# One block-inverse solve behind keys times state in a chunked delta rule, and 512-column products over [high | low] token sums in a feed-forward layer

## The chip, the cores and the metric

The kernel runs on one NeuronCore of a Trainium2 chip. Its engines work side by side and meet through semaphores: TensorE (PE, matrix products into PSUM), VectorE (DVE), ScalarE (ACT), GpSimd (POOL), and SyncE (SP), which issues most of the transfers. The metric is the device time of one execution in microseconds (us).

## The reference, cut to what matters

One layer of a streaming encoder on 512 tokens of width 1024, all in fp32: a half-step SwiGLU feed-forward (d_ff = 2816), a token mixer, a second half-step feed-forward. Each starts with an adaptive RMS norm; each result is added to x under a gate. Half of the mixer is latent attention, the other half a gated delta rule with 4 heads of 128 x 128 state, in chunks of 64 tokens in the reference (the kernel takes 128). The parts that the change touches:

```python
def _swiglu(h, w_in, w_out):
    gate, up = jnp.split(h @ w_in, 2, axis=-1)
    return (jax.nn.silu(gate) * up) @ w_out
...
    M = A + jnp.eye(CHUNK, dtype=A.dtype)
    rhs = jnp.concatenate([v * beta[..., None], k * (beta * jnp.exp(G))[..., None]], axis=-1)
    W = lax.linalg.triangular_solve(M, rhs, left_side=True, lower=True, unit_diagonal=True)
    u, wk = W[..., :GDN_DV], W[..., GDN_DV:]
...
    def step(state, inp):
        u_c, wk_c, qd_c, kd_c, qk_c, gl_c = inp
        v_new = u_c - jnp.einsum('bhck,bhkv->bhcv', wk_c, state)
        o_c = jnp.einsum('bhck,bhkv->bhcv', qd_c, state) + jnp.einsum('bhcs,bhsv->bhcv', qk_c, v_new)
        state = state * gl_c[..., None, None] + jnp.einsum('bhck,bhcv->bhkv', kd_c, v_new)
        return state, o_c
```

So u = M⁻¹(beta v), wk = M⁻¹(beta e^G k), and v_new = u − wk·S. By linearity v_new = M⁻¹(beta v − beta e^G (k·S)) as well.

## The kernel before, in words

**Arithmetic.** Every large product is made of three matmuls (mm3, L264 to L269): each operand x is kept as a high part xh, x cast to fp32r (a rounded fp32), and a low part xl = x − xh; the product is wh·xh + wh·xl + wl·xh. ACT makes the casts (L193, L804), DVE the low parts (L198, L809).

**Stages.** The first feed-forward with its down projection runs to about 410 us of the span, the mixer's projections, convolutions, attention and block inverses to about 615, the recurrence and the output projection to about 680, the second feed-forward from there to the end.

**The recurrence** (`solve`, `recur`, `gated_out`, and the loop at the end of the mixer). The kernel works on NB = 4 blocks of 128 tokens. inv[p] is the inverse of block p (its last products are L1639 and L1642). `solve(p)` computes uu = inv·vb (L1685) and, for p > 0, w = inv·kbg (L1694), both copied to SBUF; kbg and kd are scaled copies of the keys. `recur(p)` computes pw = w·S (L1711), vn = uu − pw (L1713), pq = q·S (L1719), and after a yield the state's update pst = kd·vn (L1726), S = Sg + pst (L1731; Sg, the decayed state, is made by POOL), po = qk·vn (L1734), and o = o + po (L1738). `gated_out(p)` normalises o: squares hn on ACT (L1772), their sums gs on DVE (L1773), ve (L1748), an inverse root ry on POOL (L179), on = o·ry (L1232), then four transposes of on on PE (L1757) and three operations for each head that store the high and low parts mh, ml. Beside it `fill` issues the output projection over rows that are ready (L267 to L269 with mh, ml): fill.step(3) at each yield of recur, which is nine 512-column matmuls. The loop runs with `matmuls_in_order`: PE's matmuls stay in the written order, the other engines' work is ordered by the scheduler. Each engine runs its own list strictly in order.

**The second feed-forward** (`ffn2_rest`). 22 column tiles of the hidden layer: 4 are done plainly, 18 in a fast scheme that saves an eighth of the products: with the tokens in two halves and the width in two halves, a gate and an up tile (a "pair") take 7 half-size products instead of 8. Its operands are sums of weights (x, y from g and u, `sums`), and sums of tokens t1 to t4 (`token_sums`, made once). Each product is 4 k-steps of three 256-column matmuls (L872, L873, L874). Results lie in two PSUM tiles of 512 columns, A and BC; ACT copies A out at three moments (`early_copy`, L816), DVE adds BC (`both` L822, `gate0` L825, L832), then SiLU, products and splitting. A table of due steps sets the order: pairs start 7 steps apart, their weights are loaded 11 steps ahead, their products stand at steps 0, 1, 3, 4, 6, 9 and 12, and between them stand k-steps of the down projection (512 columns, L267 to L269 with ah, al) as fill. All engines keep the written order here (`in_order`). PSUM has 3 banks of `acc` (names pa) and 5 of `aux` (names pb).

## Time and profile before

| | |
|---|---|
| time, median of 3 runs | 1047.45 us (1047.32 to 1048.46) |
| the profiled execution | 1047.25 us; span 1045.6 us |
| PE busy | 1029.0 us, 98% of the span, 6379 matmuls |
| DVE busy | 682.6 us, 65% |
| ACT busy | 448.6 us, 43% |
| POOL busy | 48.2 us, 5% |
| granted TensorE clock | 0.999 |

The span is the time between the first and the last instruction of the profile; 1.65 us of the execution lie around it. A row of a timeline gives the start in us, the duration in us, the engine, the line, and the tiles (out <- in); in brackets stands how long the engine had been idle and what released it. A row of the windows view gives a stretch, its length, and for PE, weight loads, DVE, ACT and POOL the busy time and the number of instructions, then the granted clock and the DMA share.

### The profile page before, as it was taken

What the parts mean: (1) busy time and instruction counts of PE and PEld (TensorE: products, weight loads), DVE (VectorE), ACT (ScalarE), POOL (GpSimd) and SP (SyncE); (2) the same over time, 40 slices, a digit from 0 to 9 for tenths busy, and PEclk for the clock granted to TensorE, in tenths of its full rate; (3) what the DMA queues carried; (4) which work ended last, traced back from release to release, by engine and by line L of the source; (5) the groups of instructions that cost most, each with busy time, mean ns of one, the idle gap of its engine ahead of it and who ended that gap; (6) DMA issues with size and microseconds to landing.
All of it is one profiled execution on the core that took longest, in us unless ns stands there. A gap on an engine that the chain in (4) does not pass through costs nothing.

```text
span 1045.6 us, 16109 instructions
## 1 busy us (share of the span) xinstructions
PE 1029.0 (98%) x6379; PEld 882.2 (84%) x6379; DVE 682.6 (65%) x1251; ACT 448.6 (43%) x781; POOL 48.2 (5%) x113
## 2 busy tenths in 40 slices
PE   6999999999999999999999999999999999999998
PEld 4778878788887799888778779998999999999986
DVE  4488984333486636648878556788778778777633
ACT  4343222232222226749565464465345444344422
POOL 1000000000000011100010111310000000000000
PEclk9999999999999999999999999999999999999999
DMA  9989973323586439712212201173423334333222
GB/s 274 292 232 322 298 218 101 100 84 94 190 285 220 155 102 231 185 40 54 69 41 56 72 22 41 41 162 101 141 81 102 104 99 121 91 92 109 74 61 81
DMA packets 203689, 136.88 MB, mean 131 GB/s; under 512 B 13777, under 2 KB 186590, under 8 KB 203614
## 3 DMA queue, kind: packets, MB, share of 16 engines
q1 hardware_dynamic: 202318, 131.14, 42.6%
q0 software_dynamic: 1296, 4.72, 2.4%
q8 instruction: 50, 0.82, 0.3%
q14 instruction: 25, 0.20, 0.1%
HBM read 128.63 MB, written 2.49 MB: 125 GB/s over the span
## 4 chain that ended last, share of the span: by engine, by line
PE 90%; ACT 4%; DVE 4%; issue 1%; DMA 1%; POOL 0%; SPq 0%; POOLq 0%; ACTq 0%; DVEq 0%
PE pa L267 20%; PE pa L268 20%; PE pa L269 20%; PE pb L872 6%; PE pb L873 6%; PE pb L874 6%; PE pb L267 1%; PE pb L268 1%; PE pb L269 1%; PE pb L1909 1%; PE pb L418 1%; PE pb L1939 1%; PE pb L1494 1%; DVE cv L1438 1%; PE pb L1912 1%
## 5 line engine op out<-in xcount | busy, mean ns | idle before, releaser
L267 PE MATMUL pa<-hh,wh 128*128 128x512 f32 (+1 forms) x565 | 216.8, 384 | 0.4 <-ACT hh L465 0.4
L193 ACT CAST wh<-wr 128x1024 fp32r<-128x1024 f32 (+1 forms) x106 | 107.9, 1018 | 250.6 <-PE pa L268 177.8
L268 PE MATMUL pa<-hl,wh 128*128 128x512 f32 (+1 forms) x565 | 214.7, 380 | 0.5 <-DVE hl L457 0.3
L269 PE MATMUL pa<-hh,wl 128*128 128x512 f32 (+1 forms) x565 | 214.5, 380 | 0.0
L198 DVE TENSOR_TENSOR wl<-wr,wh 128x1024 fp32r<-128x1024 f32 (+1 forms) x97 | 114.2, 1178 | 104.0 <-ACT wh L193 101.6
L267 PE MATMUL pa<-ah,wh 128*128 128x512 f32 (+1 forms) x396 | 145.5, 368 | 0.6 <-DVE xT L899 0.4
L268 PE MATMUL pa<-al,wh 128*128 128x512 f32 (+1 forms) x396 | 144.5, 365 | 0.0
L269 PE MATMUL pa<-ah,wl 128*128 128x512 f32 (+1 forms) x396 | 143.5, 362 | 0.0
L267 PEld LDWEIGHTS pa<-hh,wh 128*128 128x128 f32 x565 | 106.4, 188 | 23.9 <-issue 3.3
L269 PEld LDWEIGHTS pa<-hh,wl 128*128 128x128 f32 x565 | 106.3, 188 | 20.6 <-issue 0.9
L268 PEld LDWEIGHTS pa<-hl,wh 128*128 128x128 f32 x565 | 106.5, 188 | 19.6 <-DVE hl L457 1.1
L269 PEld LDWEIGHTS pa<-ah,wl 128*128 128x128 f32 x396 | 74.8, 189 | 12.0
L267 PEld LDWEIGHTS pa<-ah,wh 128*128 128x128 f32 x396 | 75.2, 190 | 10.3 <-ACT wh L193 1.7
L268 PEld LDWEIGHTS pa<-al,wh 128*128 128x128 f32 x396 | 75.2, 190 | 7.2
L577 DVE SCALAR_TENSOR_TENSOR aa<-ar,sc,aa 128x512 f32<-128x512 f32 x98 | 72.9, 747 | 8.2 <-DMA ar<-in_w_ada 6.8
L872 PE MATMUL pb<-fh,wh 128*128 128x256 f32 x144 | 40.7, 283 | 0.0
L874 PE MATMUL pb<-fh,wl 128*128 128x256 f32 x144 | 40.7, 283 | 0.0
L874 PE MATMUL pb<-hh,wl 128*128 128x256 f32 x144 | 40.7, 283 | 0.0
L873 PE MATMUL pb<-fl,wh 128*128 128x256 f32 x144 | 40.7, 282 | 0.0
L873 PE MATMUL pb<-hl,wh 128*128 128x256 f32 x144 | 40.7, 282 | 0.0
L899 DVE SCALAR_TENSOR_TENSOR xT<-pa,mod,xT 128x512 f32<-128x512 f32 (+1 forms) x40 | 29.3, 735 | 17.3 <-PE pa L269 17.3
L872 PE MATMUL pb<-hh,wh 128*128 128x256 f32 x144 | 40.6, 282 | 0.0
(445 smaller groups left out, 2003.1 us busy)
## 6 DMA issues: line engine op xcount, KB each, us to landing
wr<-in_ffn_w_in SPq DMA_DIRECT2D x82, 512.0 KB, 3.9
ar<-in_w_ada SPq DMA_DIRECT2D x48, 512.0 KB, 6.1
wr<-in_ffn_w_out SPq DMA_DIRECT2D x34, 512.0 KB, 3.9
ar<-in_w_ada SPq DMA_DIRECT2D x48, 256.0 KB, 4.8
wr<-in_w_in SPq DMA_DIRECT2D x21, 512.0 KB, 4.3
wr<-in_ffn_w_out SPq DMA_DIRECT2D x17, 384.0 KB, 3.4
wl<-wr POOLq DMA_DIRECT2D x9, 512.0 KB, 6.1
wr<-in_w_out SPq DMA_DIRECT2D x8, 512.0 KB, 3.8
```

Of the source, the lines that this page charges most:

```text
L193: self.nc.scalar.copy(hi, raw)
L198: self.nc.vector.tensor_tensor(out=lo, in0=raw, in1=hi.bitcast(F32), op=ALU.subtract)
L267: mm(out, wh, xh, start=start, stop=False)
L268: mm(out, wh, xl, start=False, stop=False)
L269: mm(out, wl, xh, start=False, stop=stop)
L418: nc.tensor.matmul(pg[32 * q:32 * q + 32, :256], self.sc[:, kc:kc + 1].to_broadcast([P, 32]), a[:, kc], start=(e == 0), stop=(e == 1), til ...
L577: nc.vector.scalar_tensor_tensor(out=acc, in0=a, scalar=sc, in1=acc, op0=ALU.mult, op1=ALU.add)
L872: mm(out, wh, xh, start=start and k == 0, stop=False, **kw)
L873: mm(out, wh, xl, start=False, stop=False, **kw)
L874: mm(out, wl, xh, start=False, stop=stop and k == 3, **kw)
L899: nc.vector.scalar_tensor_tensor(out=self.xT[t][:, ts], in0=p[:, ts], scalar=gate[:, t:t + 1], in1=self.xT[t][:, ts], op0=ALU.mult, op1=AL ...
L1438: nc.vector.scalar_tensor_tensor(out=a[:, d:], in0=p[:, :NT - d], scalar=wj(3 - d), in1=a[:, d:], op0=ALU.mult, op1=ALU.add)
```

## The change

**Mixer.** w = inv·kbg is not computed any more, nor are kbg and kd. `recur(p)` multiplies the keys with the state (pk = kT·S, L1722), DVE forms r = e^G·pk − vb for each head (L1724), and one solve follows: pu = inv·r (L1704); ACT copies −pu out as vn. kt is scaled in place where the values are made. A block thus has three yields for p > 0 and two for p = 0, and fill advances by 1, 3 and 2 units at them instead of 3 each.

**Second feed-forward.** The token sums are stored as [high | low], 256 columns each, in one tile. For the four products over token sums (s2, s3, s1, gate1) one 512-column matmul wh·[high | low] (L901) and one 256-column matmul wl·high (L902) take the place of three. The tile's two halves are added afterwards (`fold`, L832). The PSUM tiles are now A, U and G; U lies in `acc` for odd pairs. u's low part is made by ACT (negated copy) and an accumulating transfer on POOL's queue, g1's and the activation's low part, and one fold, by POOL instead of DVE.

```diff
@@ token_sums
-        fh, fl = self.slot(F32R, "fh"), self.slot(F32R, "fl")
-        for name, part in zip(names, (lo, hi)):
-            self.T[name].append((fh[:, part], fl[:, part]))
-        nc.scalar.copy(fh, t)
-        yield
-        v.tensor_tensor(out=fl, in0=t, in1=fh.bitcast(F32), op=ALU.subtract)
+        both = [self.slot(F32R, "fb") for _ in range(2)]
+        for name, x, part in zip(names, both, (lo, hi)):
+            self.T[name].append((x[:, lo], x[:, hi], x))
+            nc.scalar.copy(x[:, lo], t[:, part])
+        yield
+        for x, part in zip(both, (lo, hi)):
+            v.tensor_tensor(out=x[:, hi], in0=t[:, part], in1=x[:, lo].bitcast(F32), op=ALU.subtract)
@@ pair_tasks
                 nc.scalar.copy(r[name + "h"], r[src][:, part])
+                if name in 'u':
+                    nc.scalar.activation(r[name + "l"], r[src][:, part], AF.Copy, scale=-1.0)
+                    nc.gpsimd.dma_start(r[name + "l"].bitcast(F32), r[src][:, part], accum_op=ALU.add)
             return go
 
         def lo(name, src, part=slice(0, 2 * NT)):
             def go():
-                v.tensor_tensor(out=r[name + "l"], in0=r[src][:, part], in1=r[name + "h"].bitcast(F32), op=ALU.subtract)
+                if name not in 'u':
+                    eng = nc.gpsimd if name == "g1" else v
+                    eng.tensor_tensor(out=r[name + "l"], in0=r[src][:, part], in1=r[name + "h"].bitcast(F32), op=ALU.subtract)
             return go
 
         def early_copy(name, part):
             def go():
                 if name not in r:
                     r[name] = self.slot(s=name)
-                nc.scalar.copy(r[name][:, part], r["A"][:, :HALF])
+                out = r[name][:, part]
+                nc.scalar.copy(out, r["A"][:, L])
+                if name == "uc":
+                    fold(out, out, r["A"][:, H])
+                elif part is H:
+                    nc.scalar.copy(r["uc"][:, H], r["A"][:, H])
+                    nc.gpsimd.tensor_tensor(out=out, in0=out, in1=r["uc"][:, H], op=ALU.add)
             return go
 
+        def fold(out, a, b):
+            v.tensor_tensor(out=out, in0=a, in1=b, op=ALU.add)
+
         def both():
-            v.tensor_tensor(out=r["cc"], in0=r["cc"], in1=r["BC"], op=ALU.add)
+            for x in (L, H):
+                fold(r["cc"][:, H], r["cc"][:, H], r["G"][:, x])
+            fold(r["cc"][:, L], r["cc"][:, L], r["U"][:, L])
 
         def gate0():
-            v.tensor_tensor(out=r["uc"][:, H], in0=r["uc"][:, L], in1=r["BC"][:, H], op=ALU.add)
+            fold(r["uc"][:, H], r["uc"][:, L], r["G"][:, L])
+            fold(r["uc"][:, H], r["uc"][:, H], r["G"][:, H])
...
         def act1():
-            v.tensor_tensor(out=r["cc"][:, H], in0=r["cc"][:, H], in1=r["A"][:, :HALF], op=ALU.mult)
+            fold(r["uc"][:, H], r["uc"][:, H], r["A"][:, L])
+            v.tensor_tensor(out=r["cc"][:, H], in0=r["cc"][:, H], in1=r["uc"][:, H], op=ALU.mult)
...
         def act_low():
             al = self.slot(F32R, "al")
-            v.tensor_tensor(out=al, in0=r["cc"], in1=r["ah"].bitcast(F32), op=ALU.subtract)
+            eng = nc.gpsimd if f < FT - 2 else v
+            eng.tensor_tensor(out=al, in0=r["cc"], in1=r["ah"].bitcast(F32), op=ALU.subtract)
@@ product
         if "A" not in r:
-            r["A"], r["BC"] = self.aux(), self.aux()
+            r["A"] = self.aux()
+        if what == "up1":
+            r["U"] = self.acc() if r["odd"] else self.aux()
+        if what == "s3":
+            r["G"] = self.aux()
...
-            mm(out, wh, xh, start=start and k == 0, stop=False, **kw)
-            mm(out, wh, xl, start=False, stop=False, **kw)
+            if both is None:
+                mm(out, wh, xh, start=start and k == 0, stop=False, **kw)
+                mm(out, wh, xl, start=False, stop=False, **kw)
+            else:
+                mm(wide, wh, both, start=start and k == 0, stop=False, **kw)
             mm(out, wl, xh, start=False, stop=stop and k == 3, **kw)
@@ values, solve, recur
+            if p < NB - 1:
+                self.mul(h4(self.kt[p]), h4(self.kt[p]), self.bc(self.kcd[:, 4 * p:4 * p + 4], 4))
...
-        if p > 0:
-            kbg = self.slot(s="kbg")
-            self.mul(h4(kbg), h4(kt), self.bc(self.eG[:, c4], 4))
-        if p < NB - 1:
-            self.kd[p] = self.slot(s="kd")
-            self.mul(h4(self.kd[p]), h4(kt), self.bc(self.kcd[:, c4], 4))
...
-            nc.tensor.matmul(pu[:, hs(h)], u[:, hs(h)], vb[:, hs(h)], start=True, stop=True)
-        self.us[p] = self.slot(s="uu")
-        nc.scalar.copy(self.us[p], pu)
...
-        pw = self.aux()
-        for h in range(4):
-            nc.tensor.matmul(pw[:, hs(h)], kbg[:, hs(h)], u[:, hs(h)], start=True, stop=True)
-        self.wk[p] = self.slot(s="w")
-        nc.scalar.copy(self.wk[p], pw)
+            hs = slice(h * P, (h + 1) * P)
+            nc.tensor.matmul(pu[:, hs], u[:, hs], rhs[:, hs], start=True, stop=True)
+        nc.scalar.activation(vn, pu, AF.Copy, scale=scale)
+        return vn
...
-            vn = self.us[p]
+            vn = self.solve(p, self.vb[p], 1.0)
         else:
-            pw = self.aux()
+            eg = lambda h: self.eG[:, 4 * p + h:4 * p + h + 1]
+            pk, r = self.aux(), self.slot(s="r")
             for h in range(4):
-                nc.tensor.matmul(pw[:, hs(h)], self.wk[p][:, hs(h)], S[:, hs(h)], start=True, stop=True)
-            vn = self.slot(s="vn")
-            nc.vector.tensor_tensor(out=vn, in0=self.us[p], in1=pw, op=ALU.subtract)
+                nc.tensor.matmul(pk[:, hs(h)], kT[h][:, ts], S[:, hs(h)], start=True, stop=True)
+            for h in range(4):
+                nc.vector.scalar_tensor_tensor(out=r[:, hs(h)], in0=pk[:, hs(h)], scalar=eg(h), in1=self.vb[p][:, hs(h)],
+                                               op0=ALU.mult, op1=ALU.subtract)
...
+            yield
+            vn = self.solve(p, r, -1.0)
         yield
...
-                nc.tensor.matmul(pst[:, hs(h)], self.kd[p][:, hs(h)], vn[:, hs(h)], start=True, stop=True)
+                nc.tensor.matmul(pst[:, hs(h)], self.kt[p][:, hs(h)], vn[:, hs(h)], start=True, stop=True)
@@ the mixer's loop
-        chain.add(solving())
...
-        while self.wk[1] is None or deltas.open or deltas.todo:
+        while self.inv[0] is None or deltas.open or deltas.todo:
...
-                for _ in self.recur(p):
+                for i, _ in enumerate(self.recur(p, kT)):
                     loosely(chain, 2)
                     loosely(rest, 4)
                     if not rest.open and not rest.todo:
-                        fill.step(3)
+                        fill.step((1, 3, 2)[i])
                     gated.step(2)
```

**Where instructions move.** First PE, recurrence, block 2: the rows ahead of the four transposes of block 1's on. Before (nine fill matmuls between the last of pq = q·S and the transposes; between po of block 1 and these rows stand nine more, and w·S and q·S):

```order
L1719 MATMUL pb_6127<-S_6090,cv_4729 128x128
L267 MATMUL pa_6102<-mh_5666,wh_5912 128x512
L268 MATMUL pa_6102<-ml_5667,wh_5912 128x512
L269 MATMUL pa_6102<-mh_5666,wl_5913 128x512
L267 MATMUL pa_6102<-mh_5670,wh_5912 128x512
L268 MATMUL pa_6102<-ml_5671,wh_5912 128x512
L269 MATMUL pa_6102<-mh_5670,wl_5913 128x512
L267 MATMUL pa_6149<-mh_5182,wh_6050 128x512
L268 MATMUL pa_6149<-ml_5183,wh_6050 128x512
L269 MATMUL pa_6149<-mh_5182,wl_6051 128x512
L1757 MATMUL pb_6155<-ident_92,on_6153 128x128 x4
L1726 MATMUL pb_6173<-vn_6123,kd_5956 128x128 x4
```

Now (three fill matmuls between q·S and the transposes; between po of block 1 and these rows stand six, and k·S and q·S):

```order
L1731 MATMUL pb_6072<-S_6029,cv_4729 128x128
L267 MATMUL pa_6047<-mh_5186,wh_5938 128x512
L268 MATMUL pa_6047<-ml_5187,wh_5938 128x512
L269 MATMUL pa_6047<-mh_5186,wl_5939 128x512
L1771 MATMUL pb_6086<-ident_92,on_6084 128x128 x4
L1704 MATMUL pb_6104<-r_6061,U_5568 128x128 x4
L267 MATMUL pa_6047<-mh_5669,wh_5938 128x512
L268 MATMUL pa_6047<-ml_5670,wh_5938 128x512
L269 MATMUL pa_6047<-mh_5669,wl_5939 128x512
```

Nine of the eighteen fill matmuls between po and the transposes are gone from there, and the solve r·U stands behind the transposes.

Second, DVE at the same place, from the new state S to on. Before:

```order
L1731 TENSOR_TENSOR S_6090<-Sg_6038,pb_6085 128x512 [waits Pool_49]
L2121 SCALAR_TENSOR_TENSOR xT_106<-pa_6055,mod_1794,xT_106 128x512 [waits PE_49]
L1773 TENSOR_REDUCE gs_6109<-hn_6110 128x4 [waits Activation_49]
L1713 TENSOR_TENSOR vn_6123<-uu_5965,pb_6118 128x512 [waits PE_49]
L1748 SCALAR_TENSOR_TENSOR ve_6113<-gs_6109,oe_5223 128x4 [waits DVE_49]
L1232 TENSOR_TENSOR on_6153<-o_6030,ry_6115 128x512 [waits Pool_49]
L2121 SCALAR_TENSOR_TENSOR xT_106<-pa_6102,mod_1794,xT_106 128x512 [waits PE_49]
L198 TENSOR_TENSOR wl_6309<-wr_6307,wh_6308 128x1024 [waits DMAHW4_49,Activation_49]
```

Now:

```order
L1745 TENSOR_TENSOR S_6029<-Sg_5972,pb_6024 128x512 [waits PE_49,Pool_49]
L1752 TENSOR_TENSOR o_5961<-o_5961,pb_6031 128x512 [waits PE_49]
L2127 SCALAR_TENSOR_TENSOR xT_106<-pa_6014,mod_1794,xT_106 128x512 [waits PE_49]
L198 TENSOR_TENSOR wl_6270<-wr_6268,wh_6269 128x1024 [waits DMAHW2_49,Activation_49]
L1787 TENSOR_REDUCE gs_6051<-hn_6052 128x4 [waits Activation_49]
L1724 SCALAR_TENSOR_TENSOR r_6061<-pb_6060,eG_4081,vb_5460 128x128 [waits PE_49]
L1762 SCALAR_TENSOR_TENSOR ve_6055<-gs_6051,oe_5223 128x4 [waits DVE_49]
L1724 SCALAR_TENSOR_TENSOR r_6061<-pb_6060,eG_4081,vb_5460 128x128 x3
L1260 TENSOR_TENSOR on_6084<-o_5961,ry_6057 128x512 [waits Pool_49]
```

xT and the low part wl of a later weight tile moved ahead of the sums gs, and the first row of r ahead of ve.

Third, PE in the last pair: behind its product s1 (y with the last token sum) the down projection's last parts. Before, from s1's last matmul on:

```order
L874 MATMUL pb_9792<-fh_6924,yl_9728 128x256
L267 MATMUL pa_9902<-ah_9655,wh_9830 128x512
L268 MATMUL pa_9902<-al_9678,wh_9830 128x512
L269 MATMUL pa_9902<-ah_9655,wl_9831 128x512
L267 MATMUL pa_9902<-ah_9807,wh_9830 128x512
L268 MATMUL pa_9902<-al_9827,wh_9830 128x512
L269 MATMUL pa_9902<-ah_9807,wl_9831 128x512
L267 MATMUL pa_9938<-ah_9329,wh_9868 128x512 [waits Activation_49]
L268 MATMUL pa_9938<-al_9352,wh_9868 128x512
L269 MATMUL pa_9938<-ah_9329,wl_9869 128x512 [waits DVE_49]
```

Now:

```order
L902 MATMUL pb_9669<-fb_6909,yl_9613 128x256
L267 MATMUL pa_9772<-ah_9538,wh_9709 128x512
L268 MATMUL pa_9772<-al_9566,wh_9709 128x512
L269 MATMUL pa_9772<-ah_9538,wl_9710 128x512
L267 MATMUL pa_9772<-ah_9683,wh_9709 128x512
L268 MATMUL pa_9772<-al_9706,wh_9709 128x512
L269 MATMUL pa_9772<-ah_9683,wl_9710 128x512
L267 MATMUL pa_9809<-ah_9226,wh_9745 128x512 [waits DVE_49,Activation_49]
L268 MATMUL pa_9809<-al_9254,wh_9745 128x512
L269 MATMUL pa_9809<-ah_9226,wl_9746 128x512
```

The eighth row's accumulator begins with a wait for DVE now: its bank is that of U of this last pair, which is free after this row of DVE (the last one here), the third of the folds of `both`:

```order
L832 TENSOR_TENSOR uc_9608<-uc_9608,pb_9618 128x256 [waits DVE_49]
L1046 TENSOR_TENSOR wl_9783<-wr_9690,wh_9782 128x768 [waits DMAHW5_49,Activation_49]
L854 TENSOR_TENSOR cc_9543<-cc_9543,uc_9608 128x256
L832 TENSOR_TENSOR cc_9688<-cc_9688,pb_9748 128x256 [waits Pool_49]
L832 TENSOR_TENSOR cc_9688<-cc_9688,pb_9748 128x256 [waits DVE_49]
L832 TENSOR_TENSOR cc_9688<-cc_9688,pa_9693 128x256
```

These folds wait for POOL's fold of cc, which waits for two copies by ACT, which wait for s1.

More of the change, by code (lines that the diff above doesn't have):

```diff
@@ L2004, in mixer @@
         self.inv, self.ready64 = [None] * NB, [None] * NB
-        self.kd, self.us, self.o, self.wk = ([None] * NB for _ in range(4))
+        self.o = [None] * NB
         self.S = None
@@ L2041, in mixer @@
         deltas.add(self.values(vT))
-        def solving():
-            solves = Side(wide=2)
-            solves.add(*(self.solve(p) for p in range(NB)))
-            while solves.open or solves.todo:
-                solves.step(2)
-                yield
-        chain.add(solving())
         self.dense_units(4, Rates(sides, (1, 0.75, 2)), 1, z_done)
```

40 lines of the change are left out of this document (16 added, 24 removed).

## The prediction

> **What bounds the kernel now.** I read the page first, then the busy time by stretches of the span, then timelines where PE is not the whole story. From the page, the engines and the chain that ended last:
>
> ```profile
> PE 1029.0 (98%) x6379; PEld 882.2 (84%) x6379; DVE 682.6 (65%) x1251; ACT 448.6 (43%) x781; POOL 48.2 (5%) x113
> PE 90%; ACT 4%; DVE 4%; issue 1%; DMA 1%; POOL 0%; SPq 0%; POOLq 0%; ACTq 0%; DVEq 0%
> ```
>
> PE carries the span. The windows view shows whether it does so in the stages that change (recurrence, its end, then second feed-forward; columns: stretch, length, busy PE, PEld, DVE, ACT, POOL, clock, DMA):
>
> ```profile
> 615.00:660.00 45.00, 44.59 (x325) 37.24 (x326) 28.45 (x58) 20.49 (x47) 5.99 (x5) 1.00 0.12 36
> ...
> 820.00:860.00 40.00, 40.00 (x278) 37.28 (x277) 30.05 (x41) 17.70 (x29) 0.00 (x0) 1.00 0.36 107
> ...
> 980.00:1020.00 40.00, 40.00 (x255) 36.27 (x253) 17.66 (x27) 12.53 (x23) 0.00 (x0) 1.00 0.20 60
> ```
>
> PE is full in all three, so work taken from PE counts, and so does every wait of PE that did not exist. DVE at 75% (30.05 of 40) has room; POOL is idle in the feed-forward. "Busy" is no price, though, as PE's timeline there shows:
>
> ```profile
> 830.77 0.28 PE L872 MATMUL pb<-fh,yh 128*128 128x256 f32 x1
> 830.89 0.28 PE L873 MATMUL pb<-fl,yh 128*128 128x256 f32 x1
> 831.00 0.28 PE L874 MATMUL pb<-fh,yl 128*128 128x256 f32 x1
> ...
> 832.08 0.28 PE L874 MATMUL pb<-fh,yl 128*128 128x256 f32 x1
> 832.20 0.40 PE L267 MATMUL pa<-ah,wh 128*128 128x512 f32 x1
> 832.43 0.40 PE L268 MATMUL pa<-al,wh 128*128 128x512 f32 x1
> 832.67 0.39 PE L269 MATMUL pa<-ah,wl 128*128 128x512 f32 x1
> 832.90 0.28 PE L872 MATMUL pb<-hh,wh 128*128 128x256 f32 x1
> ```
>
> A 256-column matmul lasts 0.28 us but the next starts 0.119 us later (twelve from 830.77 to 832.20: 1.43 / 12). A 512-column one lasts 0.40 and the next starts 0.233 later (832.20 to 832.90: 0.70 / 3). Durations overlap; starts are the price.
>
> **The change part by part.** *1. The products with kbg go.* PE's rows for them, and po of block 1, which I need below:
>
> ```profile
> 627.97 1.06 PE L1694 MATMUL pb<-U,kbg 128*128 128x128 f32 x8
> 628.78 0.47 PE L267 MATMUL pa<-mh,wh 128*128 128x512 f32 x1
> ...
> 635.21 1.95 PE L1694 MATMUL pb<-U,kbg 128*128 128x128 f32 x16
> 636.91 0.47 PE L267 MATMUL pa<-mh,wh 128*128 128x512 f32 x1
> ...
> 644.30 1.06 PE L1734 MATMUL pb<-vn,qk 128*128 128x128 f32 x8
> 645.11 0.47 PE L267 MATMUL pa<-mh,wh 128*128 128x512 f32 x1
> ```
>
> From start to the next start: 0.81 + 1.70 = 2.5 us, with the joints 2.6 at most. Keys times state and r's solve cost what w·S and uu's product did. **−2.6 us.** The copies of w, the subtraction and the scalings that go lie on ACT and DVE, beside PE.
>
> *2. Wide products.* Four products of 18 pairs, 4 k-steps each: 288 times three narrow matmuls (3 × 0.119 = 0.358) become a wide and a narrow (0.233 + 0.119 = 0.352, or with the 0.116 that the first narrow one after a wide one shows at 832.90 rounded 0.349). 288 × (6 to 10 ns) = 1.7 to 2.9; I take the upper end, **−2.8 us**, with −1.4 to −4.4 as ends (5 ns either way, the rounding of a start). The columns stay 768 for a k-step; only one start in three goes.
>
> [...]
>
> DVE per pair: the low parts of u (1.22), g1 (0.69) and the activation (0.69) go, folds come. PE per pair takes 84 × 0.119 + 24 × 0.233 = 15.6 us (8 k-steps of fill), DVE 30.05 / 40 × 15.6 = 11.7. The rows:
>
> ```profile
> L809 DVE TENSOR_TENSOR wl<-wr,wh 128x1024 fp32r<-128x1024 f32 x18 | 21.9, 1218 | 0.2 <-ACT wh L804 0.2
> L841 DVE TENSOR_TENSOR al<-cc,ah 128x512 fp32r<-128x512 f32 x18 | 12.4, 690 | 1.9 <-ACT ah L837 0.7
> L832 DVE TENSOR_TENSOR cc<-cc,pb 128x256 f32<-128x256 f32 x18 | 7.4, 412 | 2.8 <-PE pb L874 2.8
> L816 ACT COPY cc<-pb 128x256 f32<-128x256 f32 x36 | 13.2, 367 | 5.7 <-PE pb L874 5.5
> L481 POOL TENSOR_TENSOR na<-na,sq 128x256 f32<-128x256 f32 x9 | 7.8, 868 | 112.0 <-ACT sq L479 111.9
> L196 POOL DMA_DIRECT2D wl<-wr x9 | 7.9, 878 | 36.1 <-ACT wl L195 36.1
> ```
>
> Off DVE −2.60, on it about four more folds of 0.41 (+1.7): about 10.8 of 15.6. POOL gets 0.88 (issue) + 0.87 (fold) + two 512-column subtractions. In the middle of a pair the new waits (A's halves, G, U's bank) have 3 to 7 steps, over 5 us of other products, before PE needs them: nothing, unless DVE or POOL falls behind (rival below).
>
> *3. PE stalls in the recurrence.* The transposes of on stand in PE's list before the solve, and half of the fill between po and them is gone. How long po to on takes is in the timeline for block 1:
>
> ```profile
> 645.39 0.69 DVE L1738 TENSOR_TENSOR o<-o,pb 128x512 f32<-128x512 f32 x1
> ...
> 646.17 0.63 ACT L1772 ACTIVATE hn<-o 128x512 f32<-128x512 f32 x1 [0.91 <-DVE o L1738]
> ...
> 647.46 0.68 DVE L1773 TENSOR_REDUCE gs<-hn 128x4 f32<-128x512 f32 x1
> ...
> 648.96 0.15 DVE L1748 SCALAR_TENSOR_TENSOR ve<-gs,oe 128x4 f32<-128x4 f32 x1
> 649.19 1.01 POOL L179 TENSOR_TENSOR ry<-ve,mhalf 128x4 f32<-128x4 f32 x1 [1.19 <-DVE ve L1748]
> ...
> 650.23 0.69 DVE L1232 TENSOR_TENSOR on<-o,ry 128x512 f32<-128x512 f32 x1 [1.12 <-POOL ry L179]
> 650.39 1.06 ACT L193 CAST wh<-wr 128x1024 fp32r<-128x1024 f32 x1
> ...
> 651.50 1.22 DVE L198 TENSOR_TENSOR wl<-wr,wh 128x1024 fp32r<-128x1024 f32 x1
> ```
>
> From po's start at 644.30: o after 1.09, hn 0.78 later, gs at best 0.70 later (here DVE was late), 0.70 for gs, 0.23 to ry, 1.04 to on, 0.88 to the transposes (651.11): 5.4 us. PE's cover is now po 0.81, six fill matmuls 1.40, k·S 0.89 and q·S 0.81, three fills 0.78: 4.7. It was 6.8. So blocks 1 and 2 stall 0.7 each; block 0 keeps nine fills there and stalls not; the last block has 0.81 + 15 fills (3.50) = 4.3 and stalls 1.1. For block 1 the cast of a weight tile (1.06) stands before hn on ACT, and xT and wl (1.22) before gs, one r row (0.3) before ve: gs starts 1.5 later and ve 0.3, 1.8 more. Sum 0.7 + 1.8 + 0.7 + 1.1 = 4.3, less the one stall there now:
>
> ```profile
> 659.85 0.66 PE L1757 MATMUL pb<-ident,on 128*128 128x128 f32 x4 [0.41 <-DVE on L1232]
> ```
>
> **+3.9 us**; ends: +0.5 if a fill more or a faster chain covers the plain blocks and half the detour, +5.5 if the detour happens in two blocks. Queued behind PE's wait are the solve, the fill and all later products.
>
> *4. Join of inverses and recurrence.* A copy Y by ACT stands between L1639 and L1642; before, two fill matmuls cover each (the row below: 0.37 for the copy; L1642 starts 0.67 after it starts). Now two of the four have none:
>
> ```profile
> 622.03 0.37 ACT L1654 COPY Y<-pb 64x256 f32<-64x256 f32 x1 [1.72 <-PE pb L1639]
> ```
>
> **+1.0 us** (0 to 2 × 0.67 = 1.3).
>
> *5. The tail.* The down projection's next bank waits for the third fold of `both` in the last pair. After s1's end: about 0.2 to ACT, two copies (0.27 + 0.37), POOL's fold 0.87, three folds of DVE (3 × 0.38), about 0.3 between engines: 3.1 us, against six fill matmuls (1.40) in front: **+1.5** (0.5 to 2.3, if PE's slack is smaller or POOL slower).
>
> Sum: −2.6 − 2.8 + 3.9 + 1.0 + 1.5 = +1.0 on the profiled execution's 1047.25 (span 1045.6 and 1.65 around it): 1048.25. The median of the runs lies 0.2 above that execution, so I forecast **1048.4 us**; its own range is 1046 to 1050.5.
>
> **The rivals.** *The covers hold (faster).* On, Y and U arrive in time and only parts 1 and 2 count: 1047.45 − 5.4 = 1042.0, with half a microsecond of leftovers 1042.5. For it: in block 1 before, gs waited for DVE 0.6 us and ve for vn, which is not in front any more; the scheduler may also give the cast another place in time than its list suggests. Against: the plain chain alone is 0.7 longer than the cover.
>
> *DVE and POOL slow each other (slower).* This kernel shows it when a POOL operation and DVE ones meet, Sg beside on, against the same operations alone (1.04 and 0.69):
>
> ```profile
> 640.28 1.96 POOL L1232 TENSOR_TENSOR Sg<-S,gl 128x512 f32<-128x512 f32 x1
> ...
> 641.86 0.93 DVE L1232 TENSOR_TENSOR on<-o,ry 128x512 f32<-128x512 f32 x1
> ...
> 646.96 1.04 POOL L1232 TENSOR_TENSOR Sg<-S,gl 128x512 f32<-128x512 f32 x1 [4.72 <-DVE S L1731]
> ```
>
> POOL then has 0.88 + 0.87 + 2 × 1.96 = 5.7 per pair, and what meets it on DVE takes a third longer: 10.8 + 5.7 / 3 = 12.7, still under 15.6. It decides only where each POOL operation holds DVE for its whole time: with Sg's mean of 1.5, POOL has 0.88 + 0.87 + 3.0 = 4.8, and 10.8 + 4.8 = 15.6 puts DVE level with PE; each pair is then late by some 0.3 (two folds' slowing, 0.24 each, in part hidden), 18 × 0.3 = 5.4: 1047.25 + 5.4 + 1.0 = 1053.6. [...]
>
> *All waits at their upper ends (slower).* Detours in two blocks, both Y copies bare, POOL slow in the tail: 5.5 + 1.3 + 2.3 − 5.4 = +3.7, 1051.2.
>
> *Durations are the price (much faster).* 288 × (3 × 0.28 − 0.40 − 0.28) = −46 us, 1001. The starts quoted above contradict it.
>
> **How the numbers follow.** Forecast 0.44, covers hold 0.27, contention 0.16, upper ends 0.12, durations 0.01. A measurement of this kernel tells about 0.2% (2.1 us) from no change, so the forecast is "same": 0.44; faster 0.28, slower 0.28. The range 1042.0 to 1053.0 reaches into the first rival and the contention case; about a quarter of the one, half of the other and the durations stay outside (0.07 + 0.08 + 0.01).
>
> **What would show each step.** Starts of L901 and L902 0.35 us apart per k-step (part 2). No L1694 products, and PE idle before L1771 released by DVE on, largest (2 us or more) in one block (part 3). PE idle at L1670 released by ACT (part 4), and before the down projection's L267 released by DVE near the end (part 5). Wrong: PE idle at L901 inside the pairs released by DVE or POOL (contention); no bracket at the transposes (covers hold); busy of DVE above 14 of each 15.6 us.

## The result, and the profile after

The changed kernel takes 1053.28 us (median of 6 runs, 1051.33 to 1057.53) against 1048.12 (6 runs, 1047.32 to 1049.54): ratio 1.0061, 95% interval 1.0048 to 1.0073 (the two medians alone give 1.0049). It is slower by 0.5 to 0.6%, and its runs lie further apart than those of before. The profiled execution took 1054.12 us, span 1052.4.

The busy times on its page:

```profile
PE 1026.7 (98%) x6067; PEld 866.8 (82%) x6067; DVE 704.7 (67%) x1303; ACT 467.2 (44%) x822; POOL 126.6 (12%) x183
```

There are 312 matmuls fewer, and yet the span ends 6.8 us later: the time went into waits and, as will be seen, into a lower clock. The windows view shows in which stages (columns as before: stretch, length, PE, PEld, DVE, ACT, POOL, clock, DMA share, GB/s):

```profile
618.00:621.00 3.00, 3.00 (x13) 1.75 (x14) 0.65 (x3) 2.96 (x8) 0.00 (x0) 0.63 0.00 0
...
780.00:820.00 40.00, 36.77 (x226) 33.06 (x226) 32.98 (x50) 21.46 (x37) 12.56 (x12) 0.96 0.47 119
860.00:900.00 40.00, 40.00 (x236) 35.25 (x235) 35.67 (x49) 20.61 (x36) 11.01 (x10) 1.00 0.57 146
980.00:1020.00 40.00, 38.51 (x225) 33.71 (x224) 24.24 (x43) 15.00 (x29) 9.26 (x8) 1.00 0.35 92
```

PE was full in all of these before. It now idles 3.2 us between 780 and 820 and 1.5 us near the end, and the granted clock, 1.00 in these stretches before, is low in two of them. DVE, which was to become lighter, is busy 35.67 of 40 us where it was busy 30.34 before. Four places account for the loss.

**The recurrence.** These are the rows of PE's timeline for the transposes of `on`, one for each of the four blocks:

```profile
635.31 0.63 PE L1771 MATMUL pb<-ident,on 128*128 128x128 f32 x4 [0.43 <-DVE on L1260]
...
646.38 0.63 PE L1771 MATMUL pb<-ident,on 128*128 128x128 f32 x4 [1.83 <-DVE on L1260]
...
656.00 0.66 PE L1771 MATMUL pb<-ident,on 128*128 128x128 f32 x4 [0.37 <-DVE on L1260]
...
664.75 0.66 PE L1771 MATMUL pb<-ident,on 128*128 128x128 f32 x4 [0.82 <-DVE on L1260]
```

Their idle times add up to 3.45 us, against 0.41 before.

**The join ahead of it.** PE's list of before has one to three 512-column matmuls between most groups of small products there; now the small ones stand together:

```profile
614.08 0.95 PE L1625 MATMUL pb<-ti,at 32*32 32x32 f32 x48
614.95 0.73 PE L267 MATMUL pa<-mh,wh 128*128 128x512 f32 x2
615.61 1.79 PE L1636 MATMUL pb<-ti 32*32 32x32 f32 x64
617.34 0.63 PE L1646 MATMUL pb<-ident,U 64*64 64x64 f32 x8
...
623.42 0.27 PE L1670 MATMUL pb<-U,Y 64*64 64x64 f32 x1 [0.34 <-ACT Y L1682]
...
624.45 0.27 PE L1670 MATMUL pb<-U,Y 64*64 64x64 f32 x1 [0.35 <-ACT Y L1682]
```

The waits for Y are 0.34 and 0.35 us; the larger loss is the clock, 0.63 in the stretch from 618 to 621 us and 0.80 in the next 3 us, right behind 4 us with two 512-column matmuls. In windows of 0.5 us it is 0.50 from 619.0 to 622.0, with 0.78 and 0.81 in the windows beside: 3.4 us at half clock, which cost an estimated 1.7 us (half of that length).

**The pairs near 800 us.** All engines in order of time (SPq is the queue of transfers; two issues in one row run from the first one's start to the second one's end):

```profile
799.08 7.25 SPq L118 DMA_DIRECT2D wr<-in_ffn_w_in  x2
...
800.07 0.86 POOL L808 DMA_DIRECT2D wl<-wr  x1 [1.02 <-ACT cc L847]
...
800.68 1.57 POOL L861 TENSOR_TENSOR al<-cc,ah 128x512 fp32r<-128x512 f32 x1
...
800.85 1.69 DVE L851 TENSOR_TENSOR cc<-cc,uc 128x256 f32<-128x256 f32 x1
...
809.77 1.21 DVE L789 TENSOR_TENSOR sx<-wr,wr 128x512 f32<-128x512 f32 x1 [3.23 <-DMA wr<-in_ffn_w_in]
...
812.04 0.41 DVE L854 TENSOR_TENSOR cc<-cc,uc 128x256 f32<-128x256 f32 x1
...
812.48 0.62 ACT L856 CAST ah<-cc 128x512 fp32r<-128x512 f32 x1 [4.10 <-DVE cc L854]
...
813.01 0.36 ACT L823 COPY cc<-pb 128x256 f32<-128x256 f32 x1
...
813.43 0.80 PE L901 MATMUL pb<-fb,wh 128*128 128x512 f32 x1 [3.23 <-ACT cc L823]
```

Read from the end: PE waits for ACT's copy, which stands behind a cast, which waits for DVE's product (L854), which stands in DVE's list behind the weight sum sx and one low part, and sx waits for the load of u. SP issued that load at 805.96 (the row's start plus its length, less 0.37 for the issue), 6.9 us after g's. POOL's accumulating transfer, issued at 800.07, reads the raw weights from such a buffer (wr). The DMA view of that moment has, with the time from issue to landing at the end:

```profile
wl<-wr POOLq DMA_DIRECT2D x1, 512.0 KB, 5.8
```

So it landed at about 805.8, and the next load of u went out within 0.2 us of that. The landing times in the trace make it no accident: of the 17 such transfers after 740 us, 16 are followed by a load 0.13 to 0.16 us after they have landed. In the kernel before, the two loads of a pair stand closer together:

```profile
806.73 4.54 SPq L118 DMA_DIRECT2D wr<-in_ffn_w_in  x2
```

From 794 to 935 us such rows are 4.5 to 5.8 us long there; in the changed kernel, from 812 to 960 us, they are 8.0 to 9.1. The matmul at 813.43 then takes 0.80 instead of 0.40: after the stall the clock is 0.50 from 813.5 to 816.5 in windows of 0.5 us (0.83 and 0.75 in those beside), again 3.4 us at half clock and an estimated 1.7 us.

**The tail.** The first matmul of the down projection's next bank:

```profile
1010.89 0.39 PE L269 MATMUL pa<-ah,wl 128*128 128x512 f32 x1
1012.77 0.47 PE L267 MATMUL pa<-ah,wh 128*128 128x512 f32 x1 [1.49 <-ACT cc L847]
```

In DVE's list the third fold of `both`, which reads U's bank, ends 0.15 us before that matmul starts:

```profile
1012.21 0.41 DVE L832 TENSOR_TENSOR cc<-cc,pa 128x256 f32<-128x256 f32 x1
```

PE's row names ACT's SiLU (L847), which ends at about the same time, so these rows alone do not decide between the two; combo1 below does.

### The profile page after: what moved, and what is told of

It reads as the page before. It is cut to its first block, busy times and chain, and to the rows that moved or that the text cites. A ratio compares the mean times of both kernels' runs of the same rounds, so it can differ in the third digit from the quotient of the medians.

```text
span 1052.4 us, 15754 instructions
## 1 busy us (share of the span) xinstructions
PE 1026.7 (98%) x6067; PEld 866.8 (82%) x6067; DVE 704.7 (67%) x1303; ACT 467.2 (44%) x822; POOL 126.6 (12%) x183
## 4 chain that ended last, share of the span: by engine, by line
PE 88%; DVE 4%; ACT 3%; DMA 2%; issue 2%; POOL 1%; SPq 0%; POOLq 0%; ACTq 0%; DVEq 0%
PE pa L267 20%; PE pa L268 20%; PE pa L269 20%; PE pb L901 6%; PE pb L902 5%; PE pb L899 2%; PE pb L898 2%; PE pb L267 1%; PE pb L268 1%; PE pb L269 1%; PE pb L1522 1%; PE pb L1923 1%; PE pb L418 1%; PE pb L1953 1%; DMA vb<-in_gdn_a_log 1%
## 5 line engine op out<-in xcount | busy, mean ns | idle before, releaser
L901 PE MATMUL pb<-fb,wh 128*128 128x512 f32 x144 | 53.1, 403 | 3.2 <-ACT cc L823 3.2
L832 DVE TENSOR_TENSOR uc<-uc,pb 128x256 f32<-128x256 f32 x72 | 29.9, 415 | 29.5 <-ACT uc L823 16.6
L902 PE MATMUL pb<-fb,wl 128*128 128x256 f32 x144 | 40.7, 283 | 0.0
L844 ACT ACTIVATE uc<-uc 128x256 f32<-128x256 f32 x18 | 7.5, 418 | 70.0 <-DVE uc L832 70.0
L623 DVE TENSOR_TENSOR af<-sg,pa 128x512 f32<-128x512 f32 x19 | 13.0, 685 | 35.3 <-PE pa L269 35.3
L901 PEld LDWEIGHTS pb<-fb,wh 128*128 128x128 f32 x144 | 27.6, 192 | 9.9 <-ACT cc L823 3.4
```

What stands on the lines that cost most here:

```text
L832: v.tensor_tensor(out=out, in0=a, in1=b, op=ALU.add)
L901: mm(wide, wh, both, start=start and k == 0, stop=False, **kw)
L902: mm(out, wl, xh, start=False, stop=stop and k == 3, **kw)
```

## The experiments

Times are medians; each kernel's ratio is to the kernel before on the same chip. "Idle time" is PE's time in brackets in the profile of that kernel. One profile was kept of each, so a place is known for the profiled run alone; of the other runs only the time and the mean clock are known.

| kernel | us (lowest to highest) | ratio (95%) |
|---|---|---|
| ffn2_only | 1051.53 (1051.22 to 1053.67) | 1.0038 (1.0025 to 1.0051) |
| mixer_only | 1050.39 (1047.18 to 1057.61) | 1.0032 (1.0008 to 1.0056) |
| ulow_dve | 1052.38 (1048.30 to 1056.43) | 1.0039 (1.0019 to 1.0060) |
| early_u | 1061.78 (1053.87 to 1063.62) | 1.0117 (1.0078 to 1.0156) |
| late_transposes | 1050.77 (1048.36 to 1055.74) | 1.0031 (1.0015 to 1.0046) |
| fill_join | 1051.15 (1048.93 to 1053.87) | 1.0030 (1.0020 to 1.0041) |
| spread_down | 1050.27 (1048.33 to 1057.22) | 1.0037 (1.0017 to 1.0058) |
| combo1 | 1042.82 (1041.82 to 1043.53) | 0.9951 (0.9937 to 0.9966) |
| combo_lows | 1042.13 (1041.62 to 1043.39) | 0.9946 (0.9931 to 0.9960) |
| combo_u | 1040.03 (1039.73 to 1040.40) | 0.9924 (0.9909 to 0.9939) |
| mixer_fixed | 1043.50 (1043.16 to 1045.81) | 0.9956 (0.9939 to 0.9972) |
| combo_dve | 1041.21 (1041.01 to 1041.95) | 0.9940 (0.9926 to 0.9953) |

### Each part alone

ffn2_only takes the diff's first four pieces (token_sums, pair_tasks, product), mixer_only the rest.

> Only the second feed-forward's part of the change, on the mixer of before. Theory A (a late weight load: u's raw buffer is held until the accumulating transfer has landed, the next load of u on SP waits for it, DVE's weight sums wait for that load, and PE loses 3 to 5 us at one or two places): -2.8 for the wide products, +1.5 to 1.7 for the tail, +3 to +5 for the stalls, so 1.7 to 4 us above before (1049 to 1052), with a spread of several us between runs, and an idle time of over 1 us on PE at an L901-type product. Rival B (the stall in the feed-forward comes from the changed order at the mixer's end): no such stall here, about 1.2 us below before (1046.8).

> Only the mixer's part, with the feed-forward of before. From the trace of the changed kernel: -2.6 for the products that go, +3.5 for the waits before the transposes, +2.5 at the join, -1.5 in the stretch ahead of it: about 1.9 above before (1049.5 to 1050.5), the spread of the runs as before's. Rival B (the mixer sets off the feed-forward's stall): 1052 or more, with an idle time of PE over 1 us after 740 us of the span.

ffn2_only is 4.0 above before, with an idle time of 3.2 us at the same product near 813 us and the tail's wait: the stall belongs to the feed-forward's part. The expected spread of several us did not come (2.5 us).

mixer_only has the median that was expected, but by luck: no run lies near it. Five of its runs lie between 1047.2 and 1048.9 with a mean granted clock of 1.000, five between 1051.9 and 1057.6 with 0.992 to 0.994. The profiled one is of the second kind. Its windows at the join:

```profile
615.00:618.00 3.00, 2.78 (x70) 1.99 (x63) 2.58 (x9) 2.92 (x7) 0.00 (x0) 0.84 0.00 0
618.00:621.00 3.00, 3.00 (x12) 1.81 (x11) 0.00 (x0) 2.67 (x7) 0.00 (x0) 0.50 0.00 0
...
630.00:633.00 3.00, 3.00 (x16) 2.64 (x16) 1.39 (x3) 1.04 (x1) 0.00 (x0) 0.50 0.00 0
633.00:636.00 3.00, 3.00 (x18) 2.79 (x17) 1.51 (x2) 1.09 (x2) 0.00 (x0) 0.81 0.24 70
```

The clock is halved from about 617 to 634 us while PE is busy for 2.75 us or more of every 3. So the mixer's part has two results: without the halved clock it is level with before, with it it costs 4 to 10 us. Of the 20 runs of before beside these kernels one has 0.996 (1050.72 us), the others 0.998 or more; beside all twelve kernels it is 4 runs of 59, each 2 to 3 us above the median. So before is not free of a low clock, but no trace shows where in those runs it was.

### The late load

ulow_dve, against the changed kernel:

```diff
-                if name in 'u':
-                    nc.scalar.activation(r[name + "l"], r[src][:, part], AF.Copy, scale=-1.0)
-                    nc.gpsimd.dma_start(r[name + "l"].bitcast(F32), r[src][:, part], accum_op=ALU.add)
...
-                if name not in 'u':
-                    eng = nc.gpsimd if name == "g1" else v
+                eng = nc.gpsimd if name == "g1" else v
```

> The changed kernel with the low part of u made by DVE again, as before (no negated copy, no accumulating transfer); all else as changed. Theory A: the raw buffer is free when DVE has read it, the loads of u are issued 1 to 4 us after those of g instead of 8, no stall at a product over token sums: about 5 below the changed kernel, 1048 to 1049, runs within 2 us of each other. Rival C (DVE and POOL in each other's way make DVE the bound): DVE gets 1.22 us more per pair, so 1054 to 1060.

The median misses the expectation, for a reason that it had left out: six of the ten runs have a mean clock of 0.992 to 0.995, and the profiled one, which is among them, has it halved at the join for 10.2 us. The four others lie between 1048.3 and 1049.2, as theory A said, and rival C's 1054 to 1060 is not seen in them; four of the low-clock runs lie in that range, so it falls for good only with combo_dve below, where DVE does all of this work and takes no longer than 1042. The loads of a pair stand close together again:

```profile
800.67 3.79 SPq L118 DMA_DIRECT2D wr<-in_ffn_w_in  x2
```

In PE's timeline the idle time near 810 us shrank from 3.23 to two shorter ones:

```profile
810.81 0.39 PE L894 MATMUL pb<-hh,yh 128*128 128x256 f32 x1 [0.47 <-ACT uc L823]
813.33 0.50 PE L897 MATMUL pb<-fb,wh 128*128 128x512 f32 x1 [0.83 <-ACT cc L819]
```

So the late load explains about 2 of the 3.2 us, not all.

early_u moves one entry of the table of due steps:

```diff
-(-6, hi("u", "u"))
+(-7, hi("u", "u"))
```

> The changed kernel with u's high part, negated copy and accumulating transfer one step (2.2 us) earlier in the table of due steps; no work is added or removed. Theory A: the buffer comes free about 2 us earlier, the stall of 3.2 us shrinks to about 1 or goes: 1049 to 1051. Rival C: DVE's and POOL's work is unchanged, so 1052 to 1054 as the changed kernel.

A clear miss: its median is 8 us above the changed kernel's. PE waits twice in its profile, now also for the transfer itself (queue, POOL and PE):

```profile
801.02 9.42 SPq L118 DMA_DIRECT2D wr<-in_ffn_w_in  x2
...
801.05 0.86 POOL L808 DMA_DIRECT2D wl<-wr  x1
...
809.98 0.39 PE L902 MATMUL pb<-hh,wl 128*128 128x256 f32 x1 [1.93 <-DMA wl<-wr]
...
817.22 0.79 PE L901 MATMUL pb<-fb,wh 128*128 128x512 f32 x1 [2.90 <-ACT cc L823]
```

The transfer was issued in the same moment as g's load, and PE could use its result only at 809.98, 8.9 us later; so the buffer came free later, not earlier. The next load of u went out at 810.08, 0.13 us after the transfer had landed and 9.1 us after g's. So the time to landing is not a constant, as this expectation had it: 5.8 us in the changed kernel at this place, 8.9 here. PE also loses about 0.25 us in each of the later pairs. But much of the 8 us is clock: three of the four runs have a mean of 0.988 to 0.993, and in the profiled one it is halved for 10.2 us at the join and 6.8 behind the second stall, 17.0 in all against 6.8 in the changed kernel, which costs 5 us. The one run at 1.000 takes 1053.87, 2.5 above the changed kernel's lowest.

spread_down slows the first group of the down projection, so that the pairs near 800 us have fill:

```diff
-        d0 = down(0, 4, 1, 1.3)
+        d0 = down(0, 4, 1, 0.9)
```

> The changed kernel with the first group of the down projection spread over the steps 1 to 36 of the feed-forward (rate 0.9 for 1.3), so that the pairs around 780 to 820 us have fill and stand 15 us apart instead of 11.5; no work added or removed. Theory D (the load of u, DVE and POOL need about 13 us per pair and fail only where the pairs come closer): the stall of 3.4 us with its halved clock goes, 4 to 5 below the changed kernel, 1048 to 1049 in runs without the halved clock in the mixer. Rival A alone (each load of u is late by the transfer's landing, whatever the spacing): the stall stays or moves, 1052 to 1054.

Five of its ten runs (clock 0.999 or more) lie between 1048.3 and 1049.4, as theory D said; the others have a mean clock of 0.992 to 0.998. The idle time near 810 us, with the accumulating transfer still there, is

```profile
808.71 0.50 PE L901 MATMUL pb<-fb,wh 128*128 128x512 f32 x1 [0.83 <-ACT cc L823]
```

Theory D had the stall gone; it shrank to 0.83. So it takes both: a chain (transfer, buffer, load, weight sum) that is longer than before, and pairs that come too close for it. ACT's SiLU of uc, once per pair, shows how close, in the changed kernel:

```profile
795.43 0.42 ACT L844 ACTIVATE uc<-uc 128x256 f32<-128x256 f32 x1 [3.72 <-DVE uc L832]
...
805.97 0.42 ACT L844 ACTIVATE uc<-uc 128x256 f32<-128x256 f32 x1 [2.97 <-DVE uc L832]
```

That is 10.5 us, where pairs with fill take 15.4 to 15.6; in spread_down the closest pairs are 12.4 apart. Close pairs alone are not enough: the kernel before has them too,

```profile
792.63 0.42 ACT L826 ACTIVATE uc<-uc 128x256 f32<-128x256 f32 x1 [3.39 <-DVE uc L825]
...
802.71 0.42 ACT L826 ACTIVATE uc<-uc 128x256 f32<-128x256 f32 x1 [2.02 <-DVE uc L825]
```

10.1 us apart, and PE is busy there for 39.96 of 40 us. What is new is the late load. A further buffer for u would be another test of the held buffer; it was not tried.

### The recurrence and the join

late_transposes:

```diff
-                    gated.step(2)
+                    gated.step(1 if i == 0 and p else 2)
```

> The changed kernel with the transposes of on placed behind the solve and nine fill matmuls in blocks 1 to 3, nothing else. Theory (the waits at the transposes are real time): the three waits of 0.6, 2.0 and 0.5 us go, 1 us at the last block stays; 3 us below the changed kernel run for run, so about 1048.5 in a run without the halved clock, 1050 in the median, with the halved clock at about 618 us of the span still there in some runs. Rival (the waits only move to the new value's products or to the join): within 1 us of the changed kernel.

The first three waits, 2.63 us, are gone. A part came back: the wait before the last block's transposes grew from 0.82 to 1.57, and a new one of 0.18 for the state S stands before k·S, so 1.75 of the 3.45 us are left. The median is 2.5 below the changed kernel and the lowest run 3.0 below its lowest, but the clocks differ (three of ten runs at 0.997 or less, against four of six), so these differences are not the waits alone.

fill_join:

```diff
-            chain.step(2)
+            chain.step(1)
             deltas.step()
             rest.step(4)
```

> The changed kernel with one step instead of two of the chain of inverses per turn of the loop ahead of the recurrence, so that more fill matmuls stand between the 32 x 32 and 64 x 64 products there. Theory G (the TensorE clock is halved when a few us hold little but those small products, which the changed order brought together): no halved clock at 615 to 635 us in any run, mean clock 0.998 or more, spread under 2 us, the Y waits shorter by about 1: 1050 to 1051.5 (the feed-forward's stall stays). Rival (the clock falls for a reason outside of the order): still runs of 0.991 to 0.996, median 1053.

In its profile the join runs at clock 1.00, and the waits for Y are gone. The median is as expected, but four of eight runs still have 0.993 to 0.996 and the spread is 4.9 us, which was not. In the profiled one (0.993) the low clock lies elsewhere: 6.8 us at half clock at the very start (14 to 24 us) and 6.8 behind the stall near 812 us. So this kernel alone does not settle theory G. The five kernels that follow, which hold this edit and no long stall, speak for it: all 21 of their runs have 0.999 or 1.000. They also hold late_transposes, and all but mixer_fixed spread_down; but late_transposes alone has the clock halved at the join for 10.2 us in its profile, and spread_down alone has five of ten runs at 0.992 to 0.998. What these runs do not tell is what the clock reacts to.

### The edits together, and what POOL's work costs DVE

combo1 holds late_transposes, fill_join and spread_down, and U of the last pair in the other PSUM pool (`self.acc() if r["odd"] and not r["end"]`).

> Late transposes, fill at the join and the spread down projection together, and U of the last pair in the other PSUM pool. If all four readings hold and add up: 1051.3 (the changed kernel's run without halved clock in the mixer) - 3.1 - 1 (last block, more fill) - 1 (join) - 4.5 (feed-forward) - 1.6 (tail) = 1040 to 1042, 0.6% below before, spread under 2 us. If the waits only move: 1046 or more.

It takes 1042.82 us, 0.49% below before, with a spread of 1.7 us: 0.8 above the expected range, about the wait near 805 us that is left (0.83). The tail's wait is gone, and this is what shows that it was for U's bank: of the edits only the move of U touches it (late_transposes, fill_join and spread_down each still have 1.5 us there).

Then three variants of combo1. combo_lows sets `eng = v` for the low parts of g1 and of the activation; combo_u makes ulow_dve's edit; combo_dve makes both.

> combo1 with the low parts of g1 and of the activation made by DVE again (POOL keeps its fold and the transfer). Theory (POOL and DVE block each other for whole operations, so moving these two to POOL gained DVE nothing): DVE's busy time in the feed-forward rises by less than the 1.4 us per pair that it takes over, POOL's falls by 3; PE's one remaining wait of 1 us near 805 us shrinks or stays: 1041.5 to 1043.5. Rival (DVE is relieved by POOL as counted): DVE's busy time rises by the full 1.4 us per pair (25 us) and PE waits grow: 1044 or more.

> combo1 with the low part of u made by DVE again, no accumulating transfer. If the late load of u is behind the remaining 1 us near 805 us: 1041 to 1042. If DVE's 1.22 us more per pair count once the pairs are evenly spaced: 1043.5 or more.

> combo_u with the low parts of g1 and of the activation made by DVE too: of the work that the change gave to POOL only the fold of cc is left. Theory (POOL's operations hold DVE for their whole length): DVE takes 25 us of work back and its busy time between 700 and 1010 us stays within 5 us of combo_u's 257; PE waits for nothing there, 1039.5 to 1040.5. Rival (the work counts in full): DVE above 275 of 310, PE waits in the pairs, 1041 or more.

The windows from 700 to 1010 us of combo1, combo_lows, combo_u and combo_dve, in this order:

```profile
700.00:1010.00 310.00, 309.04 (x1810) 272.32 (x1809) 246.67 (x366) 155.53 (x263) 79.18 (x70) 1.00 0.50 129
```

```profile
700.00:1010.00 310.00, 308.96 (x1808) 272.44 (x1807) 242.06 (x398) 157.13 (x262) 33.03 (x36) 1.00 0.50 130
```

```profile
700.00:1010.00 310.00, 310.00 (x1812) 273.69 (x1812) 257.31 (x382) 141.50 (x243) 71.51 (x52) 1.00 0.34 99
```

```profile
700.00:1010.00 310.00, 309.89 (x1811) 273.32 (x1810) 261.12 (x416) 140.21 (x243) 17.91 (x18) 1.00 0.33 99
```

combo_lows gives DVE about 32 operations of 0.69 us back, 22 us, and DVE's busy time falls by 4.6; between combo_u and combo_dve it rises by 3.8 for 34 operations. So the work that was moved to POOL had made DVE's other operations longer by an estimated 20 to 27 us (34 × 0.69 − 3.8 and 22 + 4.6), as much as it relieved. For PE it made no difference: combo_lows still waits 0.89 us near 805 us (and its median is within combo1's spread), combo_u and combo_dve do not wait there. What that wait needed was u's load, as combo_u shows; expected were 1041 to 1042, measured 1040.03, so the edit gained more than that wait. combo_dve has DVE's busy time as expected (261 against 257), but takes 1041.21, above the expected 1040.5 and 1.2 above combo_u on another chip; PE idles only 0.11 us more in these windows, and the rest is not explained.

combo_u is the fastest version found, 7.7 us below before on the same chip.

> The mixer's part with late transposes and fill at the join, on the feed-forward of before. The products that go (2.6 us) then count in full, with about 0.5 us gained at the last block: 1044.5 to 1045.5, spread under 2 us; so combo1's remaining 2 us are the wide products. If it is 1043 or less, the second feed-forward's part adds nothing even with its stall gone.

mixer_fixed is 4.2 below before, more than the 2.2 to 3.2 expected; its spread is 2.6 us, more than the 2 expected, because of the profiled run (1045.81), which is 2.6 us late already at 406 us of the span, ahead of every edit. By the medians combo1 is 0.7 us below it, combo_u 3.5. The profiles tell the parts more cleanly. From PE's L445 near 406 us to the next near 680 (the mixer) before takes 272.6 us, mixer_fixed and the four combos 268.5 to 268.8. From there to the end before and mixer_fixed take 366.7, combo1 365.2 and combo_u 363.5: that is what the second feed-forward's part is worth with its late load and without, 1.5 and 3.2 us, of which 2.4 are the starts of the wide products (below). The slower rate of the down projection was not run on the feed-forward of before, so a part of the rest may be its.

## Why the prediction was wrong

I forecast "no change", 1048.4, with 1042 to 1053 as the range; the kernel takes 1053.28, 0.3 us above the range. The steps that failed are two costs that the sum put at nothing: the load that the accumulating transfer holds back (6) and the clock at the join (4). The other terms were right or nearly so.

1. *Products with kbg, −2.6.* Right: they are gone. Where nothing new waits the mixer is 4.0 us shorter (272.6 against 268.5 to 268.8, above); 0.4 of that is the old wait, and 1.0 is not explained.
2. *Wide products, −2.8.* Right in kind, slightly too large. PE's timeline of the changed kernel in a full stretch:

```profile
876.69 0.40 PE L901 MATMUL pb<-fb,wh 128*128 128x512 f32 x1
876.92 0.28 PE L902 MATMUL pb<-fb,wl 128*128 128x256 f32 x1
877.04 0.39 PE L901 MATMUL pb<-fb,wh 128*128 128x512 f32 x1
```

   One k-step takes 0.35 us; the median over all 288 starts is 350 ns, against a mean of 358 for the three narrow ones before: 288 × 8 ns = 2.4 us. The rival that took the durations (0.68 against 0.84) is wrong by a factor of 20.
3. *PE stalls in the recurrence, +3.9.* Right in place and nearly in size: 3.45 of idle time against 0.41, or by starts (the gap from one matmul's start to the next, less the usual 0.23) 4.1 against 0.6, so +3.5. The largest is at block 1's transposes (1.83 idle, 2.0 by starts; forecast 2.5); block 0, which was to have none, waits 0.43.
4. *Join, +1.0.* The named waits are there and are smaller, 0.34 and 0.35. What failed is that I priced the missing fill only as cover for Y. Behind the same lack of fill the clock was halved: 1.7 us in the changed kernel's profile, 4 to 10 us in half of mixer_only's runs. It is no term of my sum.
5. *Tail, +1.5.* Right: 1.49, 1.65 by starts, and the cause is U's bank, as combo1 shows, though PE's row names ACT and not DVE.
6. *"In the middle of a pair the new waits [...] have 3 to 7 steps, over 5 us of other products [...]: nothing, unless DVE or POOL falls behind".* This is the step that failed most: 3.2 us of idle time and 1.7 of halved clock behind it. There are two errors in it. I counted when u's low part arrives, and not how long the transfer keeps its source buffer, which the next load on SP's queue needs: 4.5 to 6.5 us after the issue, and the load follows 0.14 us later. Over the second feed-forward DVE waits for that load ten times; the waits view of the changed kernel has, with total, count and longest in us:

```profile
DVE sx L789 <- DMA wr<-in_ffn_w_in: 15.7, 10, 3.2
```

   And I took 15.6 us for every pair. Between two groups of the down projection PE has no fill and a pair takes 10.5, less than DVE's 10.8. That alone was no stall before (10.1 us, with DVE at 11.7 by my count); with the late load on the chain it was.
7. *DVE at 10.8 of 15.6, contention as a rival of 0.16.* DVE is at 35.67 of 40, which is 13.9 of 15.6. The row of 1.69 us at 800.85 starts just behind the start of POOL's at 800.68 (1.57) and ends 0.3 behind its end; in the kernel before, with POOL idle, the same product (L835) takes 0.42 in the mean of its 18 rows. The 17 rows of L851 from 700 to 1010 us take 0.42 to 2.14 us, 1.36 in the mean, while the 126 folds (L832), which read one input from PSUM, take 0.41 to 0.42 like L832 before. So here DVE's product lasted through POOL's whole subtraction, where I had judged by 0.93 against 0.69; that POOL holds DVE for its whole time was an assumption of this rival, which no row of before showed. It did not decide the time: PE is full wherever pairs have fill, and combo_lows, with less work on POOL, keeps its wait. That this rival's 1053.6 is within 0.4 us of the measurement is luck: it had every pair late by 0.3 us, and the trace has one stall near 812 us and two stretches of low clock.

With their measured sizes the terms that I named give −2.6 − 2.4 + 3.5 + 0.7 + 1.5 = +0.7, 1048 us, and the runs of spread_down at clock 0.999 or more take 1048.3 to 1049.4. The stall and the two halved clocks add 3.2 + 1.7 + 1.7 = 6.6. Together 7.3, against 6.8 of span; the mixer's unexplained 1.0, and 0.7 us that the profiled run lost ahead of 406 us, leave 7.0.

## What to carry to other kernels

Here the load into a buffer that a transfer read went out 0.14 us after that transfer had landed: when a subtraction becomes an accumulating transfer, price the next load into that buffer, on the queue where it is issued, and do it for the stretch where the pieces follow each other fastest, not for their mean. Work moved from DVE to POOL brought DVE no relief here (its busy time fell by 4.6 us when combo_lows gave it 22 us of work back): count POOL's time against DVE too. And fill between small matmuls came with two things here, cover for waits (those for Y, 0.34 and 0.35 us, are gone with it) and a clock of 0.999 or more in the 21 runs that have it and no long stall; when an edit moves fill away, look at both.

## What the hardware showed that was not expected

- The TensorE clock was halved while PE was busy. In mixer_only's profile PE is busy 2.75 to 3.00 of every 3 us from 615 to 636, and the clock is 0.50 for some 17 us, behind a stretch with 112 products of 32 x 32 and few others. A low mean clock came in about half of the runs of mixer_only, ulow_dve and spread_down, which have that order and no long stall (0.992 to 0.998 against 0.999 and more), and in none of the 21 runs that have more fill between the products and no long stall. Worked out from the granted clock in windows of 2 us, the halved stretches ahead of the last 12 us of the kept profiles last 3.4 us (changed kernel, twice), 6.8 (fill_join, and early_u behind its second stall), 10.2 (ulow_dve, early_u and late_transposes at the join) or 17.1 (mixer_only), which is 1, 2, 3 and 5 times 3.4. That the small products bring the low clock about is my inference from these runs; its cause was not measured.
- An idle time of 3.2 us on PE was followed by half the clock: 512-column matmuls took 0.80 us and then 0.63 instead of 0.40, 3.4 us at half clock, an estimated 1.7 us lost. The idle times of 2.9 us in early_u (the matmul behind it takes 0.79) and 2.8 in late_transposes (clock 0.96 from 780 to 820) were followed by it too; those of 1.8 us (changed kernel, 646.38, clock 1.00 from 645 to 651) and 1.9 (early_u, 809.98; the 256-column matmuls behind it take 0.28) were not.
- The 18 accumulating transfers of 512 KB for u's low part took 4.5 to 6.5 us to land in the changed kernel, and one took 8.9 in early_u, where a load was issued in the same moment. In 16 of the 17 after 740 us the next load went out 0.13 to 0.16 us after the landing.
